# A hybrid diffusion layer on one core: the rest of the modulation summed by VectorE in place of GpSimd

## The chip, the cores and the metric

The kernel runs on one core of a Trainium2 chip. The metric is the device time of one execution in microseconds (us), the median of several runs. The engines are TensorE (PE in the rows; its weight loads are PEld), VectorE (DVE), ScalarE (ACT), GpSimd (POOL) and SyncE (SP), which here only issues DMA transfers. Each engine works through its own queue in order; the queues wait for one another by semaphores.

## The reference, cut to what matters

One layer: a modulated norm and an input projection, a token mixer (differential attention and a gated linear attention, GLA), an output projection, then a mixture of experts and a last norm. The modulation vectors come from one conditioning vector `c`:

```
mod_lat = (silu(c) @ w_ada[layer] + b_ada[layer])[:, None, :]
sh1, sc1, gt1, sh2, sc2, gt2 = split(mod_lat, 6, axis=-1)
h_lat = modulate(rms_norm(x, norm_mix_g), sh1, sc1)
y_lat, _ = token_mixer(h_lat, h_ctx, ...)
x = x + gt1 * y_lat
h2 = modulate(rms_norm(x, norm_ffn_g), sh2, sc2)
x = x + gt2 * hier_moe(h2, ...)
return rms_norm(x, final_norm_g)
```

`w_ada` is 1024 x 6144. The first 2048 columns (`sh1`, `sc1`) are needed before the first projection. The other 4096 (`gt1`, `sh2`, `sc2`, `gt2`) are needed only after the mixer; they are "the rest of the modulation" and the subject of the change.

## The kernel before, in words

All work is f32. A product is made of three matmuls on TensorE, with each operand split into an upper part `hi` (rounded, by ScalarE) and a remainder `lo` (by VectorE, one subtraction); `mm3`, lines 116 to 121, issues them, so that L119, L120 and L121 stand for nearly all multiplications. The input projection is made tile by tile by `bform` (line 446): 128 tokens by 256 (or 288) columns, 8 x 3 = 24 matmuls into a PSUM buffer `acc`, of which there are three. The weights of the projection come in pieces (`wraw`, split by L275 on ScalarE and L276 on VectorE).

The program goes through the projection in stages: GLA values (`gvalue`, 20 tiles), then in one `with` block (lines 664 to 725) the keys and gate ranks (`klr`, 10 tiles), the output gates (`r`, 16 tiles) and the queries (`q`, 8 tiles), then the values and heads of the attention (from line 848). Beside the tiles run "chains", Python generators that emit a few instructions and then yield a delay; a `Weave` ticks them after every few matmuls and so fixes by hand, with the delays of the table `DEL`, the order of the instructions on the four compute engines. SP's queue is not written by hand: a scheduler at build time sets its order.

- `klr_chain` (line 506) makes the decay gates of a tile: ScalarE (L520 to L527), VectorE (m L524, ml L529, ki L546, a copy to `sall` L552) and TensorE take turns.
- `recurrence` (line 563) carries the GLA state from chunk to chunk: dependent operations on VectorE on 64 partitions by 512 (L589, L590).
- An `r` tile: ScalarE makes the gate `gs` (L701 to L703), VectorE multiplies it with `acc` (L707) and so frees the PSUM buffer, SP stores it (L708). `gs` has two buffers. A `q` tile: VectorE multiplies `acc` with `eP` (L721), TensorE transposes the result (L657), ScalarE copies it (L659), SP stores it (L660).
- `ada_rest` (line 595) is the chain that the change touches. It makes the 4096 sums in eight parts (j) of 512 columns. Rows of `w_ada` lie eight to a partition: for each of eight k one block `aw` of 128 x 512 is loaded by SP (L603, 256 KB, three buffers), multiplied on GpSimd by the column `sil[:, 0, k]` (L643) and added to `aacc` (L645; two buffers, and the first block of a part is multiplied straight into it). After the fifth block of a part, `finish` takes up the part before: the sum is split (ah L613 on ScalarE, al L614 on VectorE), summed over the 128 partitions by two matmuls with a column of ones (L617, L618), added to the bias (brow L619) and stored (L620; some parts also in another order, L626, L631, L633). A block's load, `load()`, is emitted behind the block three places before it.

TensorE is thus tied to the chain at two points: the matmuls L617 and L618 stand in its queue and wait for the sum, and SP's queue, which loads `aw`, also carries the stores and loads of the tiles.

Of the kernel before, what the change touches and what calls it, by code (L numbers as in the profile page):

```python
# [20 lines left out]
OP = mybir.AluOpType  # L21
# [54 lines left out]
def f32(ap):  # L76
    return ap.bitcast(F32)
# [3 lines left out]
def body(ctx, tc, io, out, dbg=None):  # L81
    nc = tc.nc
# [166 lines left out]
    sil = hp.tile([P, 2, KD], F32, name="sil")  # L249
# [345 lines left out]
    def ada_rest():  # L595

        ws = []

        def load():
            i = len(ws)  # L600
            if i < 8 * KD:
                ws.append(sp.tile([P, 512], F32, name="aw", bufs=3))
                nc.sync.dma_start(ws[i], wv[:, i % KD, 2048 + i // KD * 512:2048 + (i // KD + 1) * 512])  # L603

        for _ in range(3):
            load()
        accs = {}

        def finish(j):
            acc, brow = accs.pop(j)  # L610
            ah = sp.tile([P, 512], F32R, name="ah", bufs=1)
            al = sp.tile([P, 512], F32R, name="al", bufs=1)
            nc.scalar.activation(ah, acc, AF.Copy)  # L613
            nc.vector.tensor_tensor(al, acc, f32(ah), op=OP.subtract)  # L614
            yield DEL["ar2"]
            ps = pp.tile([P, 512], F32, name="t", bufs=DEL["T"])
            nc.tensor.matmul(ps[:1], ones, ah, start=True, stop=False)  # L617
            nc.tensor.matmul(ps[:1], ones, al, start=False, stop=True)  # L618
            nc.vector.tensor_tensor(brow, ps[:1], brow, op=OP.add)  # L619
            nc.sync.dma_start(dr_mod[:, j * 512:(j + 1) * 512], brow)  # L620
            if j // 2 in (1, 2):
                c0 = j % 2 * 512
                orow = sp.tile([P, 512], F32, name="ah", bufs=1)[:1]
                src, dst = brow.rearrange("o (c k) -> o c k", k=KD), orow.rearrange("o (k c) -> o c k", k=KD)
                if j // 2 == 1:
                    nc.vector.tensor_copy(dst, src)  # L626
                else:
                    gain = sp.tile([P, 512], F32, name="al", bufs=1)[:1]
                    nc.scalar.dma_start(gain, io["ffn_g"][:, c0:c0 + 512])
                    yield DEL["ar2"]  # L630
                    nc.vector.scalar_tensor_tensor(dst, src, 1.0, gain.rearrange("o (c k) -> o c k", k=KD),  # L631
                                                   op0=OP.add, op1=OP.mult)
                nc.sync.dma_start(dr_ord[:, (j // 2 - 1) * 1024:j // 2 * 1024].rearrange(  # L633
                    "o (k c) -> o k c", k=KD)[:, :, j % 2 * 64:j % 2 * 64 + 64], orow.rearrange("o (k c) -> o k c", k=KD))

        for j in range(8):
            acc = sp.tile([P, 512], F32, name="aacc", bufs=2)
            brow = sp.tile([1, 512], F32, name="brow", bufs=2)
            accs[j] = (acc, brow)
            nc.scalar.dma_start(brow, io["b_rest"][:, j * 512:(j + 1) * 512])  # L640
            for k in range(KD):
                w = ws[j * KD + k]
                nc.gpsimd.tensor_scalar(w if k else acc, w, sil[:, 0, k:k + 1], 1.0, op0=OP.mult, op1=OP.mult)  # L643
                if k:
                    nc.gpsimd.tensor_tensor(acc, acc, w, op=OP.add)  # L645
                load()
                yield DEL["ar"]
                if k == 4 and j:
                    yield from finish(j - 1)
        yield DEL["ar1"]  # L650
        yield from finish(7)
# [12 lines left out]
    with tc.manual_schedule(engines=COMPUTE):  # L664
# [11 lines left out]
        nc.vector.tensor_copy(hmR.rearrange("p a b -> p (a b)"), raw[:, 256:456])  # L676
        sums_ps = pp.tile([P, 512], F32, name="sums", bufs=1)
        side.add(ada_rest())
        for t in range(NA):
            ps = bform("klr", t)  # L680
# [914 lines left out]
    with tc.tile_pool(name="ring_c", reuse_waits="tile", bufs=1) as ring_c, \  # L1595
# [170 lines left out]
        with tc.manual_schedule():  # L1766
# [63 lines left out]
            for n in range(2):  # L1830
                c = slice(n * 512, n * 512 + 512)
# [15 lines left out]
    with tc.For_i(0, again, 1):  # L1847
        with tc.tile_pool(name="ov", reuse_waits="tile", bufs=1) as ov, \
                tc.tile_pool(name="ov_ps", reuse_waits="tile", bufs=1, space=PSUM) as op_:

            def til(name, shape, dt=F32):
                return ov.tile([P] + list(shape), dt, name="ov" + name)

            with tc.For_i(0, n_extra, 1) as it:
# [65 lines left out]
                for i, nm in enumerate(("w_gate", "w_up")):  # L1920
                    for hf in range(2):
                        w = til("wt", [4, 512])
# [16 lines left out]
                for hf in range(2):  # L1939
                    w = til("wt", [2, 1024])  # L1940
# [118 lines left out]
```

## Time and profile before

| | |
|---|---|
| median of 3 runs | 1458.75 us (1458.16 to 1459.15) |
| the profiled execution | 1454.76 us, span 1452.9 us from first to last instruction |
| busy share of the span | PE 92%, PEld 76%, DVE 76%, ACT 60%, POOL 30% |
| instructions of DVE and POOL | 1589 and 393 |
| chain that ended last, by engine | PE 61%, DVE 11%, DMA 9%, POOL 7%, ACT 4%, issue 3% |

The times in the rows are from the start of that execution's span. Durations of TensorE are modelled and overlap, since matmuls are pipelined; a new one of 256 columns starts much sooner than the one before is shown to end. "Idle before" and the releaser in brackets tell how long an engine stood and what ended it; a wait for several things is put down to the last. PEclk is the granted clock of TensorE as a share of 2.4 GHz; its lower level is 1.2 GHz.

### The profile page before, as it was taken

What the parts mean: (1) busy time and instruction counts of PE and PEld (TensorE: products, weight loads), DVE (VectorE), ACT (ScalarE), POOL (GpSimd) and SP (SyncE); (2) the same over time, 40 slices, a digit from 0 to 9 for tenths busy, and PEclk for the clock granted to TensorE, in tenths of its full rate; (3) what the DMA queues carried; (4) which work ended last, traced back from release to release, by engine and by line L of the source; (5) the groups of instructions that cost most, each with busy time, mean ns of one, the idle gap of its engine ahead of it and who ended that gap; (6) DMA issues with size and microseconds to landing.
All of it is one profiled execution on the core that took longest, in us unless ns stands there. A gap on an engine that the chain in (4) does not pass through costs nothing.

```text
span 1452.9 us, 21094 instructions
## 1 busy us (share of the span) xinstructions
PE 1332.4 (92%) x7352; PEld 1105.0 (76%) x7352; DVE 1102.2 (76%) x1589; ACT 870.4 (60%) x1458; POOL 437.5 (30%) x393
## 2 busy tenths in 40 slices
PE   6898987899999899999899599999999999999982
PEld 1698886889888788887688467777777777777761
DVE  5553568734765699999556689999999999999975
ACT  6744753223222488888443467777777777777781
POOL 1576578810234434433100202222222222222201
PEclk9799999899999999999999699999999999999996
DMA  8526665676546961512574689999999999999963
GB/s 275 198 91 179 191 202 159 218 244 192 166 149 188 246 184 44 138 44 85 212 260 155 237 330 355 372 369 369 375 378 370 375 363 358 358 372 362 351 268 150
DMA packets 121539, 360.77 MB, mean 248 GB/s; under 512 B 18726, under 2 KB 47422, under 8 KB 98388
## 3 DMA queue, kind: packets, MB, share of 16 engines
q1 hardware_dynamic: 109808, 337.50, 66.4%
q0 software_dynamic: 10080, 20.09, 5.0%
q10 hardware_dynamic: 1540, 1.78, 0.4%
q8 instruction: 59, 0.97, 0.3%
q14 instruction: 52, 0.43, 0.1%
HBM read 318.24 MB, written 58.74 MB: 259 GB/s over the span
## 4 chain that ended last, share of the span: by engine, by line
PE 61%; DVE 11%; DMA 9%; POOL 7%; ACT 4%; issue 3%; SPq 0%; POOLq 0%; DVEq 0%; ACTq 0%
PE acc L119 4%; PE acc L121 4%; PE acc L120 4%; PE y L119 4%; PE y L121 4%; PE y L120 4%; PE u L120 4%; PE u L121 3%; PE g L119 3%; PE g L121 3%; PE u L119 3%; PE g L120 3%; POOL aacc L645 3%; PE y L1676 3%; DVE nm L1037 3%
## 5 line engine op out<-in xcount | busy, mean ns | idle before, releaser
L1628 DVE TENSOR_TENSOR lo<-ring,hi 128x1024 fp32r<-128x1024 f32 x323 | 382.8, 1222 | 43.0 <-ACT hi L1627 28.6
L1627 ACT ACTIVATE hi<-ring 128x1024 fp32r<-128x1024 f32 x323 | 335.7, 1059 | 87.1 <-PE y L121 53.3
L119 PE MATMUL acc<-whi,hThi 128*128 128x256 f32 (+1 forms) x592 | 178.2, 301 | 7.9 <-DVE gs L707 5.4
L121 PE MATMUL acc<-whi,hTlo 128*128 128x256 f32 (+1 forms) x592 | 172.5, 291 | 0.9 <-DVE hTlo L326 0.6
L120 PE MATMUL acc<-wlo,hThi 128*128 128x256 f32 (+1 forms) x592 | 171.9, 290 | 0.4 <-DVE wlo L276 0.3
L119 PEld LDWEIGHTS acc<-whi,hThi 128*128 128x128 f32 x592 | 117.1, 198 | 9.8 <-DVE gs L707 5.8
L121 PEld LDWEIGHTS acc<-whi,hTlo 128*128 128x128 f32 x592 | 116.5, 197 | 2.5 <-DVE hTlo L326 2.1
L120 PEld LDWEIGHTS acc<-wlo,hThi 128*128 128x128 f32 x592 | 116.6, 197 | 2.0 <-DVE wlo L276 0.8
L119 PE MATMUL u<-hi,xh 128*128 128x512 f32 x256 | 100.9, 394 | 3.5 <-ACT hi L1627 3.5
L120 PE MATMUL u<-lo,xh 128*128 128x512 f32 x256 | 100.9, 394 | 3.5 <-DVE lo L1628 3.5
L119 PE MATMUL g<-hi,xh 128*128 128x512 f32 x256 | 103.8, 405 | 0.0
L120 PE MATMUL g<-lo,xh 128*128 128x512 f32 x256 | 100.6, 393 | 0.8 <-DVE lo L1628 0.8
L121 PE MATMUL g<-hi,xl 128*128 128x512 f32 x256 | 100.8, 394 | 0.0
L121 PE MATMUL u<-hi,xl 128*128 128x512 f32 x256 | 100.4, 392 | 0.0
L1037 DVE TENSOR_REDUCE nm<-S 128x1 f32<-128x1280 f32 x64 | 94.9, 1485 | 6.1 <-PE S L1032 6.1
L1032 PE MATMUL S<-kst,qst 128*128 128x512 f32 (+1 forms) x384 | 93.2, 380 | 4.5 <-ACT p L1042 3.4
L1042 ACT ACTIVATE p<-S,nm 128x1280 f32<-128x1280 f32 x64 | 85.0, 1328 | 15.4 <-DVE nm L1037 10.9
L1607 POOL DMA_INDIRECT xg<-dr_h,tok x32 | 45.2, 1414 | 149.7 <-DVE tok L1252 127.7
L119 PE MATMUL y<-hi,th 128*128 128x512 f32 x186 | 85.2, 458 | 0.0
L645 POOL TENSOR_TENSOR aacc<-aacc,aw 128x512 f32<-128x512 f32 x56 | 79.9, 1428 | 4.7
L1032 PEld LDWEIGHTS S<-kst,qst 128*128 128x128 f32 x384 | 66.0, 194 | 17.7 <-ACT p L1042 7.7
L121 PE MATMUL y<-hi,tl 128*128 128x512 f32 x186 | 72.6, 390 | 0.0
(399 smaller groups left out, 3267.5 us busy)
## 6 DMA issues: line engine op xcount, KB each, us to landing
ring<-in_w_down_dram SPq DMA_DIRECT2D x63, 1024.0 KB
ring<-in_w_gate_dram SPq DMA_DIRECT2D x57, 1024.0 KB
ring<-in_w_up_dram SPq DMA_DIRECT2D x57, 1024.0 KB
aw<-in_w_ada_dram SPq DMA_DIRECT2D x64, 256.0 KB
wraw<-in_w_in_dram SPq DMA_DIRECT2D x44, 256.0 KB
wada<-in_w_ada_dram SPq DMA_DIRECT2D x16, 512.0 KB
qst<-dr_q SPq DMA_DIRECT2D x32, 256.0 KB
raw_o<-in_w_gate_dram SPq DMA_DIRECT2D x14, 512.0 KB
```

Source lines behind the costliest of these rows:

```text
L119: nc.tensor.matmul(out_ap, ah, bh, start=start, stop=False)
L120: nc.tensor.matmul(out_ap, ah, bl, start=False, stop=False)
L121: nc.tensor.matmul(out_ap, al, bh, start=False, stop=stop)
L645: nc.gpsimd.tensor_tensor(acc, acc, w, op=OP.add)
L1032: nc.tensor.matmul(S[:, c0:c0 + cn], st["qst"][m][s][:, qt * P:(qt + 1) * P], st["kst"][m][:, c0:c0 + cn], start=(s == 0), stop=(s == 1))
L1037: nc.vector.tensor_reduce(d["nm"][:, m:m + 1], d["S"][m], AX.X, OP.max, negate=True)
L1042: nc.scalar.activation(d["p"][m], d["S"][m], AF.Exp, bias=d["nm"][:, m:m + 1], accum_out=d["sm"][:, m:m + 1])
L1607: nc.gpsimd.indirect_dma_start(out=xgb[e % 3], out_offset=None, in_=dr_h2, in_offset=bass.IndirectOffsetOnAxis(ap=tok[:, o:o + 1], axis=0) ...
L1627: nc.scalar.activation(hi, raw, AF.Copy)
L1628: nc.vector.tensor_tensor(lo, raw, f32(hi), op=OP.subtract)
L1676: nc.tensor.matmul(y[:, n], tf[:, kk - PARTS], ws[kk][:, n * 512:(n + 1) * 512], start=start, stop=stop)
```

## The change

The multiplication by the column and the addition become one operation, scalar_tensor_tensor, on VectorE: aacc = aw x c + aacc. The first block of a part is a tensor_scalar on VectorE. Loads, yields, buffers and `finish` stay. Lines of the kernel behind L641 move down by two: the gate product L707 is L709 after, L721 is L723, L657 is L659.

```diff
             for k in range(KD):
                 w = ws[j * KD + k]
-                nc.gpsimd.tensor_scalar(w if k else acc, w, sil[:, 0, k:k + 1], 1.0, op0=OP.mult, op1=OP.mult)
+                c = sil[:, 0, k:k + 1]
                 if k:
-                    nc.gpsimd.tensor_tensor(acc, acc, w, op=OP.add)
+                    nc.vector.scalar_tensor_tensor(acc, w, c, acc, op0=OP.mult, op1=OP.add)
+                else:
+                    nc.vector.tensor_scalar(acc, w, c, 1.0, op0=OP.mult, op1=OP.mult)
                 load()
                 yield DEL["ar"]
```

The instructions move on three engines. First VectorE's queue in the r tiles, from a brow (L619) on; before:

```order
L619 TENSOR_TENSOR brow<-t,brow 1x512
L626 COPY ah<-brow 1x64x8
L707 TENSOR_TENSOR gs<-gs,acc 128x256
L589 TENSOR_TENSOR sall<-sall 64x512
L590 TENSOR_TENSOR sall<-sall,e_1349 64x512
L589 TENSOR_TENSOR sall<-sall 64x512
L590 TENSOR_TENSOR sall<-sall,e_1349 64x512
L707 TENSOR_TENSOR gs<-gs,acc 128x256 x3
```

and the same place after (L645 and L647 are the new operations):

```order
L709 TENSOR_TENSOR gs<-gs,acc 128x256
L645 SCALAR_TENSOR_TENSOR aacc<-aw,sil,aacc 128x512 x2
L589 TENSOR_TENSOR sall<-sall 64x512
L590 TENSOR_TENSOR sall<-sall,e_1349 64x512
L589 TENSOR_TENSOR sall<-sall 64x512
L590 TENSOR_TENSOR sall<-sall,e_1349 64x512
L709 TENSOR_TENSOR gs<-gs,acc 128x256
L647 TENSOR_SCALAR aacc<-aw,sil 128x512
L645 SCALAR_TENSOR_TENSOR aacc<-aw,sil,aacc 128x512
L709 TENSOR_TENSOR gs<-gs,acc 128x256
L645 SCALAR_TENSOR_TENSOR aacc<-aw,sil,aacc 128x512 x2
L709 TENSOR_TENSOR gs<-gs,acc 128x256
```

The three gates that stood side by side now have two blocks between each pair; the order of VectorE's other operations is unchanged. On GpSimd's queue the 120 operations of L643 and L645 are gone, and only the ten small memsets of `st` (L688) are left between the value stage and the attention's values.

Second, TensorE's queue where the last of the eight sums goes over the partitions (`ah` of the last part; `acc` with numbers, to tell the tiles apart); before, in the first value tile of the attention:

```order
L119 MATMUL acc_3418<-whi_3107,hThi_154 128x256
L120 MATMUL acc_3418<-wlo_3108,hThi_154 128x256
L617 MATMUL t_3393<-ah_3389,ones_75 1x512
L121 MATMUL acc_3418<-whi_3107,hTlo_155 128x256
L119 MATMUL acc_3418<-whi_3107,hThi_154 128x256
```

and after, in the third value tile (the first is acc_3362, the second acc_3412):

```order
L119 MATMUL acc_3447<-whi_3061,hThi_154 128x256
L120 MATMUL acc_3447<-wlo_3062,hThi_154 128x256
L617 MATMUL t_3337<-ah_3333,ones_75 1x512
L121 MATMUL acc_3447<-whi_3061,hTlo_155 128x256
L119 MATMUL acc_3447<-whi_3061,hThi_154 128x256
```

The matmuls of the last sum stand two tiles later in the queue; those of the seventh, and the transposes of the last query tile, about one tile later. TensorE's order is otherwise the same but for one transpose that moves by four matmuls, and ScalarE's is unchanged. On SP's queue the 64 loads of `aw` stand at other places among the same stores and loads.

## Rows read from the trace of the kernel before

**Rows 1.** By stretches: busy us (count) of PE, PEld, DVE, ACT, POOL; PEclk, DMA share, GB/s.

```profile
128.00:188.70 60.70, 55.70 (x402) 50.50 (x403) 33.06 (x54) 43.76 (x105) 39.80 (x44) 1.00 0.58 174
188.70:256.00 67.30, 53.10 (x417) 50.34 (x416) 50.42 (x66) 28.32 (x66) 51.63 (x43) 0.95 0.60 181
256.00:286.80 30.80, 26.62 (x199) 25.93 (x197) 26.02 (x28) 6.29 (x11) 24.46 (x21) 0.88 0.67 216
286.80:303.00 16.20, 11.69 (x82) 10.72 (x81) 5.69 (x10) 4.15 (x8) 7.80 (x9) 0.89 0.62 201
303.00:400.00 97.00, 96.58 (x683) 89.50 (x683) 52.16 (x125) 27.31 (x88) 11.31 (x8) 1.00 0.64 203
```

**Rows 2.** Chain that ended last, 90 to 300 us: shares by line.

```profile
by line: POOL aacc L645 23.2%; POOL aw L643 14.9%; DMA aw<-in_w_ada_dram 11.5%; issue 4.2%; DMA dr_gv<-gvs 3.7%; PE acc L121 3.7%; PE acc L119 3.6%; PE acc L120 3.6%; DMA dr_gs<-gs 3.4%; POOL aacc L643 2.0%; DMA eP<-dr_eP 1.9%; DVE wlo L276
```

**Rows 3.** Groups of GpSimd, 100 to 296 us: busy us, mean ns | idle before.

```profile
L645 POOL TENSOR_TENSOR aacc<-aacc,aw 128x512 f32<-128x512 f32 x56 | 79.9, 1428 | 4.7
L643 POOL TENSOR_SCALAR aw<-aw,sil 128x512 f32<-128x512 f32 x56 | 52.3, 933 | 11.5 <-DMA aw<-in_w_ada_dram 11.5
```

**Rows 4.** Waits of PE, SP and ACT, stages before 305: us, times, longest.

```profile
PE t L617 <- ACT ah L613: 6.4, 5, 3.8
PE acc L119 <- DVE gs L707: 5.4, 2, 4.3
...
SPq L603 <- POOL aacc L645: 61.0, 35, 4.5
...
SPq L708 <- DVE gs L707: 5.1, 3, 4.4
...
ACT gs L701 <- DMA dr_gs<-gs: 27.8, 11, 4.1
```

**Rows 5.** Timeline of DVE, ACT, PE: start us, us [idle before <-releaser].

```profile
252.50 1.98 DVE L631 SCALAR_TENSOR_TENSOR ah<-brow,al 1x512 f32<-1x512 f32 x1
...
254.65 0.38 ACT L701 ACTIVATE gs<-acc 128x256 f32<-128x256 f32 x1 [3.16 <-DMA dr_gs<-gs]
...
254.79 0.58 PE L119 MATMUL acc<-whi,hThi 128*128 128x256 f32 x1 [4.25 <-DVE gs L707]
```

**Rows 6.** Timeline of DVE and POOL around 240 us.

```profile
234.21 1.67 DVE L590 TENSOR_TENSOR sall<-sall,e 64x512 f32<-64x512 f32 x1
...
239.63 0.68 DVE L590 TENSOR_TENSOR sall<-sall,e 64x512 f32<-64x512 f32 x1
240.33 0.69 DVE L589 TENSOR_TENSOR sall<-sall 64x512 f32<-64x512 f32 x1
...
242.70 0.69 POOL L643 TENSOR_SCALAR aw<-aw,sil 128x512 f32<-128x512 f32 x1 [4.58 <-DMA aw<-in_w_ada_dram]
```

**Rows 7.** DVE 128x512 in the timeline, and the group of the gate product.

```profile
144.63 0.68 DVE L546 TENSOR_TENSOR ki<-ki,kk 128x512 f32<-128x512 f32 x1
145.24 0.68 DVE L524 SCALAR_TENSOR_TENSOR m<-g,na 128x512 f32<-128x512 f32 x1
...
L707 DVE TENSOR_TENSOR gs<-gs,acc 128x256 f32<-128x256 f32 x16 | 6.5, 412 | 8.2 <-ACT gs L703 8.2
```

**Rows 8.** Groups of DVE over the whole span, and one cast in the timeline.

```profile
L1055 DVE SCALAR_TENSOR_TENSOR p<-p,kap,p 128x768 f32<-128x768 f32 x32 | 32.3, 1011 | 0.0
...
L1745 DVE SCALAR_TENSOR_TENSOR ring<-ring,n_y,raw_o 128x1024 f32<-128x1024 f32 x8 | 9.7, 1279 | 0.0
...
100.43 0.42 DVE L670 CAST mh<-m 98x512 fp32r<-98x512 f32 x1
```

**Rows 9.** Pieces of the same chain: aw loads, start us, us.

```profile
104.98 2.48 DMA aw<-in_w_ada_dram
...
237.91 4.70 DMA aw<-in_w_ada_dram
```

**Rows 10.** Timeline of PE and ACT at the tail.

```profile
293.96 0.44 PE L617 MATMUL t<-ah,ones 128*1 128x512 f32 x1 [3.83 <-ACT ah L613]
...
300.09 0.38 ACT L862 ACTIVATE dqh<-acc 128x256 fp32r<-128x256 f32 x1 [2.18 <-PE acc L121]
```

## The prediction

> **What bounds the kernel now.** I read the view by stretches first [rows 1]. From 303 to 400 us TensorE is busy 96.58 of 97 us, and the attention and expert stages behind it start only when it gets there: what is won before 303 us comes off the whole time. Between 128 and 303 us TensorE is not full. The work there falls into four stretches: the ten gate tiles ("gate", 128 to 188.7), the sixteen r tiles ("r", to 256), the eight q tiles ("q", to 286.8) and the change-over to the value tiles ("tail", to 303). TensorE is busy 55.70 of 60.70, 53.10 of 67.30, 26.62 of 30.80 and 11.69 of 16.20 us, and in the last three the granted clock sinks to 0.95, 0.88 and 0.89 of 2.4 GHz.
>
> Next, who is late. In the chain of what ended last between 90 and 300 us, the two GpSimd lines of the summation hold 23.2% and 14.9% [rows 2]. Their cost [rows 3]: 79.9 us for 56 additions and 52.3 us for the 56 scalings ahead of them, 132 us or 2.36 us a block, and eight scalings that begin a sum. The waits show how this reaches TensorE [rows 4]. Directly: it waits 6.4 us for the upper half `ah` of a finished sum. Indirectly, by two roads: SP's queue stood 61.0 us behind aw loads whose buffer GpSimd had not freed, and ScalarE waited 27.8 us for stores of `gs` in that queue; and 5.4 us for r tiles' gate products, which free PSUM, when VectorE's queue was late. One such place [rows 5]: ScalarE gets its next `gs` buffer only at 254.65 after 3.16 us, and TensorE starts again at 254.79 after 4.25 us idle, once a gate product is done that stood on VectorE behind recurrence steps and an operation of 1.98 us at 252.50.
>
> **What the change removes.** All 120 operations on GpSimd, and with them a second cost. VectorE's product L590 took 1.67 us at 234.21 and 0.68 us at 239.63; in between GpSimd ran dry (its next scaling starts at 242.70 after 4.58 us of waiting) [rows 6]. So VectorE's long durations are company of GpSimd, not work. Counted with free durations (0.61 us from start to start for independent 128x512 operations, 0.70 for the dependent 64x512 ones, 0.41 for a gate [rows 6, 7]) VectorE's own work in r is 16 gates 6.6, thirteen 128x512 operations 7.9, 22 steps of the recurrence 15.4 and 14 others of finished sums and small steps at 0.55 on average, 7.7: 37.6 us, where it is busy 50.42 [rows 1]. In q it is 14 x 0.61 + 12 x 0.70 and one other of about 1.1, 18.0 us, where it is busy 26.02.
>
> **What it adds.** 56 scalar_tensor_tensor and 8 tensor_scalar on VectorE, 128x512 f32. No row has the first in that shape from SBUF: 128x1024 costs 1.279 us, 128x768 1.011 [rows 8], by the line through both 128x512 costs 0.74; the floor is 0.61, the start distance above, the ceiling 1.011. The 0.74 is nearest, since size scales it. For a tensor_scalar I take 0.42, a cast of 98x512 [rows 8], and no more than 0.74 in any case, which would add 2.6 us over the whole. Sum 56 x 0.74 + 8 x 0.42 = 44.8 us. By the order the 64 blocks lie 2 before the gate tiles, 22 in gate, 24 in r, 12 in q, 4 in the tail. GpSimd ran ahead of its place whenever a load and a sum buffer were there; VectorE takes each block where it stands in the order.
>
> **Stretch by stretch**, with VectorE free of GpSimd:
> - gate: 20 x 0.74 + 2 x 0.42 = 15.6 us on VectorE, which is busy 33.06 of 60.70 now. TensorE is at 55.70, so little can be won. Most blocks fall where VectorE waits for ScalarE, but about one per tile stands ahead of a step of the gate chain (m, ki or ml) on which TensorE waits: at most 10 x 0.74 = 7.4. Against it, ml and ki lose their long durations and 1.3 us of a gate matmul's wait goes. Bounds -5 to +7.4, taken **+1.5**.
> - r: 37.6 + 21 x 0.74 + 3 x 0.42 = 54.4 us on VectorE, just above TensorE's 53.10. Now VectorE is the bound, and what is late next is the reload of an aw buffer. There are three buffers, so a block's load is issued when the block three before it is done; from issue to landing it takes 2.48 to 4.70 us [rows 9], taken 4.5, near the upper end, since the entry may stand behind another on SP. On average three blocks take 54.4 / 8 = 6.8 us, enough. In three places blocks of two gates stand without a recurrence step between, and VectorE needs only 2.0 to 3.0 us for three blocks: 1.5 to 2.5 us late each, 6 in all. So 54.4 + 6 = 60.4 against 67.30: **-6.9**; bounds -12.9 (no wait) and +6 (the durations do not fall).
> - q: 18.0 + 10 x 0.74 + 2 x 0.42 = 26.2 on VectorE, TensorE 26.62; the same late reloads, twice 2, and up to 2 for the eP loads in the same queue: 32.5 against 30.80: **+1.7**; bounds -4.2 and +9.
> - tail: now the last sum reaches TensorE at 293.96 and it waits 3.83 us with the first value tile half done [rows 10]; the third value tile ends near 303, one tile of 24 matmuls (at most 24 x 97 / 683 = 3.4 us by rows 1) after the second is evacuated at 300.09. After the last q product VectorE has one block, al, brow, three blocks, a wait of 0.7 for `ah` and al: 0.74 + 0.61 + 0.61 + 2.2 + 0.7 + 0.69, with 1 for late loads 6.6 us. In the new order the last two matmuls of the sum stand inside the third value tile, two tiles later than now, so TensorE has work meanwhile and ends that tile some 9 us after the last q product, not 16.2: **-7.2**; bounds -8.7 and -3.
>
> The edits with no price of their own: DMA bytes stay as they are. In the value stage ahead of 128 us SP stops less; TensorE's multiplications cover that, and without the cover it would be a gain. GpSimd's memsets for `st` come earlier, off the path. Behind 303 us the other work keeps its order, and TensorE covers it. Sum +1.5 - 6.9 + 1.7 - 7.2 = **-10.9 us**. The profiled execution took 1454.76 us (span 1452.9), 4 us under the median of the runs, so it becomes 1443.9, and the median 1458.75 becomes **1447.9**.
>
> **The rivals.**
> - *The whole gain.* Loads land in time and no chain is lengthened: gate 0, r at 54.4 (-12.9), q at TensorE's 26.6 (-4.2), tail -8.7: -25.8, 1433. For it: average spacing 6.8 us against 4.5. Against it: the bunched blocks.
> - *VectorE's queue replaces GpSimd's.* gate pays its +7.4, r waits 9 (-3.9), q 8 (+3.8), tail -7.2: +0.1, 1459. For it: both engines are within 2 us of each other in r and q, and an in-order queue hands every wait on.
> - *Slower: reloads late throughout.* VectorE stops at a block whose load is still queued on SP, and behind it stand the gate products that free PSUM. 36 blocks of r and q through three buffers are twelve rounds of reload plus 0.74. If a load also lies behind a store held as long as the longest hold of a gate store today, 4.4 us [rows 4], a round is 8.9 + 0.74: 115.7 us against 98.1 now, +17.6, with +1.5 and -7.2 gives +11.9, 1471. It decides from a reload of 7.9 us on, where the rounds eat 98.1 + 5.7. Against it: those holds came from GpSimd being behind.
> - *Slower: VectorE is full and stays so.* If the long durations were its own, r is 50.42 + 16.8 + 6 (+5.9), q 26.02 + 8.2 + 6 (+9.4); with +1.5 and -4 for the tail +12.8, 1472. Row 239.63 speaks against it. The Trainium skill's Perfetto Trace Analysis, section Optimizing Scalar/DVE Operations, points this way: from a saturated VectorE work may go to GpSimd, and since both share an SBUF read port, moving work between them might not help; this change moves it toward the fuller engine. By that rule 1472, by rows 6 the forecast.
> - *It does not do what it says:* the order shows all 64 blocks on VectorE and none on GpSimd, so no chance for this.
>
> **How the numbers follow.** A measurement of this kernel tells 0.2% (2.9 us) from no change. Chances: forecast 0.52 (its own range 1440 to 1453), the whole gain 0.12, VectorE's queue 0.17, late reloads 0.13, VectorE full 0.06. Faster 0.64, same 0.17, slower 0.19. The range 1435 to 1466 leaves out half of the whole gain and some two thirds of the slower cases, about 0.18.
>
> **What would show it.** GpSimd's 132 us gone; 56 blocks of about 0.74 us and 8 of about 0.42; L589 and L590 at 0.7; VectorE nearly full in r (over 54 of some 60 us) with waits on aw loads of a few us; the wait at the last sum gone; r some 7 us and tail some 7 shorter. It is wrong if the recurrence steps stay above 1 us, if VectorE waits over 15 us on aw loads, if gate grows by more than 5, or if what is won before 303 us is lost behind it.

## The result, and the profile after

The changed kernel takes **1444.7 us** (median of 4 runs, 1443.57 to 1445.63) against 1458.95 us of the kernel before (four runs too), a ratio of **0.991** (95% interval 0.989 to 0.993). Timed once more beside other kernels it took 1443.06 us against 1456.7, again 0.991 (0.989 to 0.993). The profiled execution took 1444.24 us with a span of 1442.4, 10.5 us less than the profiled one of before. Forecast were 1447.9 us, and -10.9 us between profiled executions.

Behind the edited lines the numbers grow by 2: the gate product L707 is now L709, ScalarE's first step on an r tile L701 is L703, the q product L721 is L723, and the evacuation of a value tile L862 and L863 is L864 and L865. By the stretches of [rows 1], each ending at the same work as before (columns as there: busy us and count of PE, PEld, DVE, ACT, POOL; the last two rows cover what follows):

```profile
126.70:189.30 62.60, 58.09 (x410) 52.45 (x409) 43.09 (x76) 44.26 (x106) 0.70 (x7) 0.97 0.60 190
189.30:247.80 58.50, 49.64 (x397) 47.13 (x396) 50.99 (x90) 27.93 (x65) 1.95 (x3) 0.94 0.68 199
247.80:278.90 31.10, 27.49 (x237) 26.66 (x236) 26.11 (x41) 7.40 (x13) 0.00 (x0) 1.00 0.86 263
278.90:287.40 8.50, 7.05 (x53) 6.36 (x53) 6.53 (x11) 2.93 (x6) 0.00 (x0) 1.00 0.57 190
287.40:300.00 12.60, 9.84 (x66) 9.26 (x67) 5.00 (x11) 2.19 (x5) 0.00 (x0) 0.86 0.91 290
300.00:400.00 100.00, 99.58 (x679) 91.21 (x678) 55.24 (x131) 28.80 (x96) 14.62 (x10) 1.00 0.61 193
```

Gate went from 60.7 to 62.6 us, r from 67.3 to 58.5, q from 30.8 to 31.1, the tail from 16.2 to 8.5: +1.9 - 8.8 + 0.3 - 7.7 = -14.3 us. The tail ends 15.6 us earlier (287.4 against 303.0), as the gate stretch also began 1.3 us earlier. But from 287.4 to 300 us TensorE is busy only 9.84 of 12.6 us, at a granted clock of 0.86 of 2.4 GHz, and gets through 66 matmuls; in the 12.6 us behind the tail of the kernel before (303.0 to 315.6) it was busy throughout, at a granted clock of 1.00, and got through 102. A part of the gain is lost there.

The chain that ended last, 90 to 300 us, which before held GpSimd's two lines with 40% (first blocks included) [rows 2]:

```profile
by line: PE acc L119 10.3%; PE acc L121 10.1%; PE acc L120 10.1%; DMA aw<-in_w_ada_dram 7.0%; DVE aacc L645 6.6%; issue 6.3%; DMA dr_gs<-gs 5.0%; PE g L550 4.5%; DMA wraw<-in_w_in_dram 2.8%; DMA eP<-dr_eP 2.3%; DMA dr_v<-dqh 2.3%; PE g L537
```

VectorE's recurrence in the kernel before, 128 to 303 us (busy us, mean ns | idle before):

```profile
L590 DVE TENSOR_TENSOR sall<-sall,e 64x512 f32<-64x512 f32 x18 | 21.5, 1192 | 0.6
L589 DVE TENSOR_TENSOR sall<-sall 64x512 f32<-64x512 f32 x16 | 17.7, 1108 | 0.1
```

and VectorE's groups after, 100 to 303 us, which answer to [rows 3, 6]:

```profile
L645 DVE SCALAR_TENSOR_TENSOR aacc<-aw,sil,aacc 128x512 f32<-128x512 f32 x56 | 41.7, 744 | 4.0 <-DMA aw<-in_w_ada_dram 3.6
L276 DVE TENSOR_TENSOR wlo<-wraw,whi 128x512 fp32r<-128x512 f32 (+1 forms) x24 | 16.8, 700 | 15.5 <-ACT whi L275 15.1
L590 DVE TENSOR_TENSOR sall<-sall,e 64x512 f32<-64x512 f32 x18 | 12.4, 686 | 0.6
L589 DVE TENSOR_TENSOR sall<-sall 64x512 f32<-64x512 f32 x16 | 10.9, 682 | 0.1
...
L529 DVE TENSOR_TENSOR ml<-m,mh 128x512 fp32r<-128x512 f32 x10 | 6.9, 687 | 2.9 <-ACT mh L527 2.8
```

An addition costs 0.744 us, and the steps of the recurrence take 0.68 to 0.69 us where their means were 1.11 and 1.19 us. The waits of SP's queue, ScalarE and TensorE, 100 to 303 us, against [rows 4]:

```profile
SPq L603 <- DVE aacc L645: 28.7, 31, 5.2
...
SPq L603 <- DVE gs L709: 8.3, 8, 3.4
...
ACT gs L703 <- DMA dr_gs<-gs: 14.6, 7, 4.2
ACT dqh L864 <- DMA dr_v<-dqh: 9.9, 3, 8.6
...
PE t L618 <- DVE al L614: 5.1, 4, 2.6
PE acc L119 <- DVE dql L865: 3.9, 2, 2.6
PE t L617 <- ACT ah L613: 2.9, 3, 1.5
```

[rows 4] begin at 128 us. From 100 us SP stood 66.2 us on the blocks' loads behind the additions in the kernel before, where the first of these rows has 28.7. New on SP are 8.3 us in which a load of a block stands behind a gate product in VectorE's queue. ScalarE waits 14.6 us for its `gs` buffers in place of 27.8. New before 303 us is the wait at `dqh` and `dql`, the evacuation of the value tiles. The timeline shows it:

```profile
284.69 0.39 ACT L864 ACTIVATE dqh<-acc 128x256 fp32r<-128x256 f32 x1 [0.28 <-issue]
285.50 0.38 ACT L864 ACTIVATE dqh<-acc 128x256 fp32r<-128x256 f32 x1
294.99 0.38 ACT L864 ACTIVATE dqh<-acc 128x256 fp32r<-128x256 f32 x1 [8.60 <-DMA dr_v<-dqh]
...
295.88 0.58 PE L119 MATMUL acc<-whi,hThi 128*128 128x256 f32 x1 [2.58 <-DVE dql L865]
```

TensorE ran ahead of the evacuations until no PSUM buffer was free, and waited 2.58 us. The evacuations of the kernel before (all twenty, then the third) and of the changed kernel (all twenty):

```profile
L862 ACT ACTIVATE dqh<-acc x20: 376/384/386, 297.0 to 363.7; 128x256 fp32r<-128x256 f32 x20
...
307.31 0.39 ACT L862 ACTIVATE dqh<-acc 128x256 fp32r<-128x256 f32 x1 [6.32 <-DMA dr_v<-dqh]
...
L864 ACT ACTIVATE dqh<-acc x20: 377/384/386, 284.7 to 352.8; 128x256 fp32r<-128x256 f32 x20
```

The first comes 12.3 us earlier than before, the third too, and the last 10.9 us earlier. The third waited for a store in both kernels.

### The profile page after: what moved, and what is told of

Read it like the earlier page. It is cut to its first block, busy times and chain, and to the rows that moved or that the text cites. A ratio compares the mean times of both kernels' runs of the same rounds, so it can differ in the third digit from the quotient of the medians.

```text
span 1442.4 us, 21048 instructions
## 1 busy us (share of the span) xinstructions
PE 1331.0 (92%) x7352; PEld 1104.1 (77%) x7352; DVE 1115.2 (77%) x1653; ACT 870.6 (60%) x1458; POOL 298.7 (21%) x273
## 4 chain that ended last, share of the span: by engine, by line
PE 68%; DVE 13%; DMA 7%; ACT 5%; issue 4%; POOL 2%; SPq 0%; ACTq 0%; POOLq 0%; DVEq 0%
PE acc L119 5%; PE acc L120 5%; PE acc L121 5%; PE y L119 4%; PE y L121 4%; PE y L120 4%; PE u L120 4%; PE g L120 4%; PE u L121 4%; PE g L121 4%; PE g L119 4%; PE u L119 4%; PE y L1678 4%; DVE nm L1039 3%; PE S L1034 2%
## 5 line engine op out<-in xcount | busy, mean ns | idle before, releaser
L120 PE MATMUL y<-lo,th 128*128 128x512 f32 x186 | 72.5, 390 | 0.0
```

Of the source, the lines that this page charges most:

```text
L120: nc.tensor.matmul(out_ap, ah, bl, start=False, stop=False)
```

## The experiments

**Theory:** most of the gain is that VectorE's own operations lose the company of GpSimd, which had made them long. **Rivals:** the gain is GpSimd's slow chain no longer holding load buffers and SP's queue; or it belongs to the tail alone, where the last sum stood in TensorE's way.

Profiled executions also differ ahead of the gate tiles and behind the start of the attention, where no edit aimed: ScalarE's first evacuation of a gate tile (`kk`) falls between 122.8 and 128.1 us in these fourteen profiles (124.7 and 122.8 in two of the changed kernel), and from the first attention score to the end of the span they take 964.0 to 971.6 us. So the kernels are compared from the one of these two landmarks to the other. For the kernel before these rows give 126.0 and 483.8, 357.8 us between, for the changed kernel 124.7 and 472.8, 348.1 us between:

```profile
L684 ACT ACTIVATE kk<-acc x10: 367/378/387, 126.0 to 180.3; 128x256 f32<-128x256 f32 x10
...
L1032 PE MATMUL S<-kst,qst x384: 276/393/722, 483.8 to 670.8; 128*128 128x512 f32 x128, 128*128 128x256 f32 x64
...
L686 ACT ACTIVATE kk<-acc x10: 365/378/387, 124.7 to 180.3; 128x256 f32<-128x256 f32 x10
...
L1034 PE MATMUL S<-kst,qst x384: 276/393/629, 472.8 to 659.9; 128*128 128x512 f32 x128, 128*128 128x256 f32 x64
```

In between stand the first `gs`, the first q product and the first `dqh`, which cut the stretches of the table. They are not those of [rows 1], in which the expectations count: the r tiles of the changed kernel are 58.5 us there and 63.5 here, those of the kernel before 67.3 and 70.6. Us by stretch, then median and ratio of the timed runs:

| kernel | gate tiles | r tiles | q tiles and change-over | values to attention | sum | median | ratio (95%) |
|---|---|---|---|---|---|---|---|
| before | 59.7 | 70.6 | 40.7 | 186.8 | 357.8 | 1456.7 to 1458.95 | 1 |
| changed | 61.0 | 63.5 | 35.5 | 188.1 | 348.1 | 1444.7 | 0.991 (0.989 to 0.993) |
| the same again | 61.0 | 63.8 | 36.5 | 187.0 | 348.3 | 1443.1 | 0.991 (0.989 to 0.993) |
| idle work on GpSimd | 65.7 | 89.4 | 40.4 | 186.7 | 382.2 | 1478.5 | 1.015 (1.013 to 1.018) |
| scaling alone | 62.1 | 69.1 | 35.1 | 188.3 | 354.6 | 1447.8 | 0.993 (0.991 to 0.995) |
| adding alone | 74.0 | 83.4 | 35.2 | 187.8 | 380.4 | 1473.6 | 1.010 (1.009 to 1.012) |
| thin sum | 58.4 | 59.6 | 32.4 | 188.1 | 338.5 | 1433.7 | 0.984 (0.982 to 0.986) |
| first 3 sums on GpSimd | 59.7 | 63.7 | 36.5 | 188.6 | 348.5 | 1443.8 | 0.991 (0.989 to 0.993) |
| last 5 sums on GpSimd | 60.6 | 71.8 | 41.5 | 186.8 | 360.7 | 1455.5 | 0.999 (0.998 to 1.001) |
| four buffers | 61.1 | 62.2 | 36.4 | 186.4 | 346.1 | 1438.9 | 0.987 (0.986 to 0.989) |
| table late | 61.0 | 63.1 | 35.7 | 186.3 | 346.1 | 1440.9 | 0.988 (0.987 to 0.990) |
| both | 60.6 | 62.9 | 34.9 | 186.0 | 344.4 | 1439.3 | 0.989 (0.987 to 0.991) |
| both, blocks closer | 61.1 | 65.5 | 33.6 | 188.1 | 348.3 | 1440.7 | 0.988 (0.986 to 0.989) |
| both, rows by GpSimd | 61.0 | 61.5 | 36.1 | 186.1 | 344.7 | 1441.0 | 0.989 (0.987 to 0.990) |

The changed kernel, profiled twice, repeats its sum to 0.2 us, single stretches to 1.1; the kernel before and each of the others were profiled once. By this the change is worth 9.5 to 9.7 us between the landmarks.

**Idle work on GpSimd.** The bias rows lie in the first row of two 128x512 tiles, whose rows 64 to 127 are the scratch.

```diff
+                nc.gpsimd.tensor_scalar(dm[1], dm[0], h_, 1.0, op0=OP.mult, op1=OP.mult)
+                nc.gpsimd.tensor_tensor(dm[0], dm[0], dm[1], op=OP.add)
                 load()
```

> The changed kernel, with GpSimd given its old 128 operations back as idle work: at each block a scaling and an adding of 64x512 zeros in scratch rows, on which nobody waits. The sum stays on VectorE. Theory (most of the gain is VectorE's own operations getting back to their undisturbed durations): VectorE's 64x512 and 128x512 operations in the stretch of the recurrence go from 0.69 us back to 1.0 to 1.2 us, the 56 summing operations from 0.75 to 1.0 us or more, the stretch of the r units grows by 8 to 15 us, and the time is 1455 to 1470 us, as slow as the kernel before or slower. Rival (the gain is that GpSimd's slow chain no longer releases the load buffers and the gate products): nobody waits for GpSimd here either, so the time stays at 1443 to 1447 us.

These are 128 idle operations; the kernel before had 120 there. It took 1478.5 us, 34 us more than the changed kernel, beyond the theory's own upper end. Groups of 120 to 310 us:

```profile
L654 POOL TENSOR_TENSOR bb<-bb,bb 64x512 f32<-64x512 f32 x58 | 89.0, 1534 | 4.8
L653 POOL TENSOR_SCALAR bb<-bb,sil 64x512 f32<-64x512 f32 x57 | 63.0, 1105 | 5.6
L649 DVE SCALAR_TENSOR_TENSOR aacc<-aw,sil,aacc 128x512 f32<-128x512 f32 x50 | 56.1, 1123 | 0.4
L590 DVE TENSOR_TENSOR sall<-sall,e 64x512 f32<-64x512 f32 x18 | 19.4, 1079 | 0.6
L589 DVE TENSOR_TENSOR sall<-sall 64x512 f32<-64x512 f32 x16 | 18.3, 1142 | 0.1
```

and by stretches, from the first `gs` to the first q product:

```profile
190.40:279.80 89.40, 64.45 (x463) 61.30 (x462) 84.42 (x95) 32.38 (x73) 83.77 (x63) 0.85 0.48 143
```

Nobody waits for this work, and yet the recurrence is back at 1.08 to 1.14 us, a summing operation takes 1.12 us, and VectorE is busy 84.42 of 89.40 us. So the company of GpSimd is shown as a cost by itself, and the rival that leaves it out falls. The run is no copy of the kernel before: there VectorE does not have the sum as well. Nor does it divide the 9.5 to 9.7 us: what part of them came from the operations' own durations, and what part from load buffers and SP's queue freed sooner, no run separates.

**Scaling alone, adding alone.** The same with one of the two lines.

> The kernel with idle work on GpSimd, but with the scaling alone: 64 operations of 64x512 at the places of before, no adding. With both, 33.9 us more than in the changed kernel passed from the start of the gate stretch to the attention (382.2 against 348.1 to 348.3 us), for 63.0 us of scaling and 89.0 us of adding on GpSimd. Theory (VectorE is disturbed for as long as GpSimd works, whatever GpSimd does): the damage goes by GpSimd's time, 8 to 18 us, and the time is 1452 to 1462 us. Rival (the adding, which reads two operands, is what disturbs): 0 to 4 us and 1442 to 1448 us.

> The same with the adding alone: 64 idle operations of 64x512 with two operands, no scaling. Theory (VectorE is disturbed for as long as GpSimd works): 14 to 24 us more than the changed kernel, 1458 to 1468 us. Rival (only the adding disturbs): nearly the whole damage, 28 to 34 us, 1471 to 1478 us.

Against 348.2 us the scaling costs 6.4 us, the adding 32.2, nearly all of the 34 of both. For the adding the rival holds; for the scaling the 6.4 us lie between the two, and the median, 1447.8 us, just inside the rival's bounds. The idle operations keep their places in GpSimd's queue, but as they wait for no block they run ahead of the sum: the last scaling starts at 208.2 us and the last adding at 240.6. By stretch their numbers are alike (32 scalings and 29 additions in the gate tiles, 25 and 27 in the r tiles), so one operation can be set against the other. VectorE's groups of 120 to 340 us, with scaling alone:

```profile
L649 DVE SCALAR_TENSOR_TENSOR aacc<-aw,sil,aacc 128x512 f32<-128x512 f32 x55 | 44.5, 810 | 4.3 <-DMA aw<-in_w_ada_dram 3.9
...
L529 DVE TENSOR_TENSOR ml<-m,mh 128x512 fp32r<-128x512 f32 x10 | 7.3, 733 | 3.0 <-ACT mh L527 2.8
```

and with adding alone:

```profile
L653 POOL TENSOR_TENSOR bb<-bb,bb 64x512 f32<-64x512 f32 x55 | 86.0, 1564 | 4.3
L649 DVE SCALAR_TENSOR_TENSOR aacc<-aw,sil,aacc 128x512 f32<-128x512 f32 x55 | 55.0, 999 | 4.5 <-DMA aw<-in_w_ada_dram 4.1
...
L529 DVE TENSOR_TENSOR ml<-m,mh 128x512 fp32r<-128x512 f32 x10 | 11.8, 1176 | 2.9 <-ACT mh L527 2.8
...
L552 DVE COPY sall<-g 128x512 f32<-128x512 f32 x10 | 6.8, 680 | 0.7 <-PE g L550 0.7
L524 DVE SCALAR_TENSOR_TENSOR m<-g,na 128x512 f32<-128x512 f32 x10 | 6.8, 680 | 0.0
...
L651 DVE TENSOR_SCALAR aacc<-aw,sil 128x512 f32<-128x512 f32 x7 | 6.6, 939 | 0.0
```

`ml`, made in the gate tiles from two operands in SBUF, goes from 0.69 to 1.18 us beside the additions and to 0.73 beside the scalings, though GpSimd is busy for much the same share of these tiles (43.8 of 74.0 us with additions, 31.6 of 62.1 with scalings). `m`, with one operand in PSUM, and the copy out of PSUM stay at 0.68 beside the same additions. The Trainium skill, SBUF — State Buffer, section Who interferes with whom, says that a VectorE instruction contends with GpSimd when it has two inputs in SBUF and GpSimd reads SBUF, and that one with at most one SBUF input, outside the two-port modes, does not. The rows of L649 and L529 (two tensors in SBUF, stretched) and of L552 and L524 (one operand in PSUM, not stretched) agree. The first block of a part, L651, reads one tensor in SBUF and a column, and it is stretched too, from 0.48 to 0.94 us; in which mode it runs no row shows. Of a difference between GpSimd's scaling and its adding that section says nothing; here it is 6.4 against 32.2 us.

**Thin sum.**

```diff
-                    nc.vector.scalar_tensor_tensor(acc, w, c, acc, op0=OP.mult, op1=OP.add)
+                    nc.vector.scalar_tensor_tensor(acc[:, :8], w[:, :8], c, acc[:, :8], op0=OP.mult, op1=OP.add)
```

> The changed kernel with the 56 adding operations cut to the first 8 of 512 columns, so most of the sum over rows is left out; loads, order and waits are kept. It gives the price of the work on VectorE. Theory (VectorE's 41.7 us are hidden behind the matmuls except in the stretch of the r units, where VectorE is busy 51.0 of 58.5 us): 3 to 8 us faster than the changed kernel, 1437 to 1442 us, most of it in the r units, which can't fall below their 49.6 us of matmuls. Rival 1 (all 41.7 us hidden): 1443 to 1446 us. Rival 2 (the loads set the pace, not VectorE): also 1443 to 1446 us, with VectorE idle on the blocks' loads for more than the 4 us of now.

The additions, 120 to 310 us:

```profile
L645 DVE SCALAR_TENSOR_TENSOR aacc<-aw,sil,aacc 128x8 f32<-128x8 f32 x55 | 12.0, 218 | 7.4 <-DMA aw<-in_w_ada_dram 7.1
```

9.7 us less by the sums, 9 to 11 by the medians: more than the theory gave. And the saving does not sit in the r units alone: gate 2.6, r 3.9 to 4.2, q and change-over 3.1 to 4.1. So the sum still costs something in each stretch: about a third of the 29 us that were taken off VectorE. The time, 1433.7 us, rules out both rivals. The sign that the second named did come, in part: with VectorE lighter, its waits for blocks grow from 3.9 to 9.9 us (7.1 at these additions, 2.8 at the first blocks).

**First and last sums on GpSimd.** `j < 3`, or `j >= 3`, decides which engine takes a block:

```diff
-                if k:
+                if j < 3:
+                    nc.gpsimd.tensor_scalar(w if k else acc, w, c, 1.0, op0=OP.mult, op1=OP.mult)
+                    if k:
+                        nc.gpsimd.tensor_tensor(acc, acc, w, op=OP.add)
+                elif k:
                     nc.vector.scalar_tensor_tensor(acc, w, c, acc, op0=OP.mult, op1=OP.add)
```

> The blocks of the first three sums of eight (24 of 64, those of the gate stretch) go to GpSimd as in the kernel before, the other 40 stay on VectorE. By stretch, the changed kernel was 1.9 us slower in the gate stretch and 8.8 us faster in the r units. Theory (each stretch pays for itself, VectorE being disturbed only while GpSimd works): the gate stretch is back at 60 to 61 us, the r units stay at 58 to 61 us, and the time is 1441 to 1446 us. Rival (GpSimd falls behind in the gate stretch and its backlog reaches into the r units, as it does in the kernel before): the r units take 62 us or more and the time is 1448 to 1456 us.

> The other way round: the blocks of the first three sums on VectorE, the other 40 on GpSimd as in the kernel before. Theory (the gain belongs to the stretches from the r units on, where GpSimd disturbs VectorE and ends the tail): the r units take 65 to 69 us again, the tail about 16 us, and the time is 1454 to 1461 us, the kernel before or a little slower. Rival (half of the gain comes from GpSimd having no backlog at the start of the r units): the r units take 61 to 64 us and the time is 1448 to 1453 us.

Both as the theory said, by the times and by the table set against the changed kernel and the kernel before. With the first sums on GpSimd the gate tiles are back at 59.7 us and the r tiles stay at 63.7; of the 1.3 us won the sum, 348.5 us, shows nothing. With the last ones there, r takes 71.8 us, q and change-over 41.5, as in the kernel before, and the gain is gone. The recurrence of this last run, 120 to 310 us:

```profile
L590 DVE TENSOR_TENSOR sall<-sall,e 64x512 f32<-64x512 f32 x18 | 22.7, 1261 | 0.6
L589 DVE TENSOR_TENSOR sall<-sall 64x512 f32<-64x512 f32 x16 | 18.2, 1135 | 0.1
```

The gain belongs to the 40 blocks behind the gate tiles, about 7 us of it to the r tiles and 4 to 5 to the q tiles and the change-over, so the tail alone does not account for it either.

**Four buffers.** The room comes from the bias row, loaded later into one buffer.

```diff
-                ws.append(sp.tile([P, 512], F32, name="aw", bufs=3))
+                ws.append(sp.tile([P, 512], F32, name="aw", bufs=4))
...
+            brow = sp.tile([1, 512], F32, name="brow", bufs=1)
+            nc.scalar.dma_start(brow, io["b_rest"][:, j * 512:(j + 1) * 512])
```

> The changed kernel with four buffers for the blocks in place of three (the room is taken from the bias row, which has one buffer in place of two and is loaded when a sum is finished). It tests the term of the late reloads, for which the prediction took 6 us in the r units, while the trace after shows VectorE waiting 4.0 us for blocks in all. Theory (the term was too large): 0 to 3 us faster, 1441 to 1445 us, with VectorE's waits for blocks under 1.5 us. Rival (the reloads hold more than the waits show, by SyncE's queue, which stands 28 us behind the summing operations): 4 to 8 us faster, 1437 to 1441 us.

The additions, 120 to 310 us:

```profile
L645 DVE SCALAR_TENSOR_TENSOR aacc<-aw,sil,aacc 128x512 f32<-128x512 f32 x55 | 40.9, 743 | 0.5
```

VectorE's waits for blocks fall from 4.0 to 0.5 us, and 2.1 us are won up to the attention: the theory's size. The median fell by 4 to 6 us, as the rival said; the kernel with both edits, below, decides between them.

**Table late.**

```diff
-        nc.scalar.dma_start(rope, io["rope"])
...
+                if (i, t) == (0, 6):
+                    nc.scalar.dma_start(rope, io["rope"])
```

> The changed kernel with the load of the 1 MB rotation table moved from ahead of the value tiles to behind the seventh of them. After the tail the trace shows 4.6 us of the gain given back between 287 and 353 us, where ScalarE waits 8.6 us at 295 us for a store of values that was issued at 290 us. Theory (the table's load, which now starts at 284 us, takes the transfer time from the loads and stores of that stretch): the wait falls under 3 us and the time falls by 2 to 4.5 us, to 1440 to 1443 us. Rival (SyncE's queue, which stands 5.2 us on the last row of the sum before it can issue the stores, holds them): the wait stays at 6 us or more and the time at 1443 to 1446 us.

The third evacuation of a value tile:

```profile
293.32 0.38 ACT L863 ACTIVATE dqh<-acc 128x256 fp32r<-128x256 f32 x1 [8.18 <-DMA dr_v<-dqh]
```

2.1 us by the sums and a median inside the theory's bounds, but not by the wait that it named: that stands at 8.2 us, as the rival said. How the 2.1 us came is open; single stretches repeat only to 1.1 us.

**Both, and the changed kernel again beside it.**

> The changed kernel itself, timed again beside the next kernels so that they stand against the same runs. All theories: 1443 to 1447 us, a ratio of 0.990 to 0.992.

> The changed kernel with both earlier edits: four buffers for the blocks, and the rotation table loaded behind the seventh value tile. Alone they gave 1438.9 and 1440.9 us; against the changed kernel the first matmul of the attention scores started 1.2 us and 3.0 us earlier. Theory (the two are local and add up, and what the four buffers gave beyond 1.2 us arose behind the attention and is not theirs): the attention starts 3.5 to 5 us earlier than in the changed kernel and the time is 1438 to 1442 us. Rival (all that was measured is theirs, and adds up): 1434 to 1437 us.

From gate tiles to attention 344.4 us, 3.8 less than the changed kernel: 2.1 and 2.1 nearly add up. The time, 1439.3 us, is 3.7 less than the changed kernel's on the same chip. The local theory holds; four buffers are not worth 6 us. It is the best version found by the sums, 0.25% under the changed kernel, though the intervals of the two ratios still overlap. Here the third `dqh` comes at 291.01 and waits for TensorE, not for a store:

```profile
291.01 0.38 ACT L863 ACTIVATE dqh<-acc 128x256 fp32r<-128x256 f32 x1 [7.83 <-PE acc L121]
```

**Both, blocks closer,** with `ar` at 1.0.

> The kernel with both edits (four buffers, table late), and the distance between two blocks of the sum cut from 1.15 to 1.0 in the order's units, so that some 13 per cent of the blocks move forward, out of the r and q units into the gate stretch, where VectorE is busy 40.9 of 60.6 us against 53.9 of 62.9 us in the r units. Theory (what is left of the sum's cost lies in the r units, where VectorE is nearly full): from the start of the gate stretch to the attention 2 to 4 us less than the 344.4 us of the kernel with both edits, and a time of 1435 to 1438 us. Rival (the gate stretch has no room either, since its waits go through VectorE as well): 0 to 2 us more, 1439 to 1442 us.

The gate and the r tiles of this run:

```profile
123.90:185.00 61.10, 56.70 (x398) 51.18 (x398) 40.97 (x72) 42.77 (x103) 0.69 (x7) 0.97 0.57 181
185.00:250.50 65.50, 56.74 (x438) 54.24 (x437) 54.59 (x95) 32.85 (x74) 1.89 (x3) 0.92 0.63 196
```

VectorE has 72 operations in the gate stretch, as many as without the edit, and 95 in r, also as many. So no block moved into the gate tiles, and the run tells nothing of its question. What it does show: up to the change-over TensorE waits 8.0 us for `al` where it waited 4.0, its granted clock in the r tiles is 0.92 where it was 1.00, and 3.9 us are lost by the sums. That the places of the finished sums did this is likely, not shown.

**Both, rows by GpSimd.**

```diff
-            nc.sync.dma_start(dr_mod[:, j * 512:(j + 1) * 512], brow)
+            nc.gpsimd.dma_start(dr_mod[:, j * 512:(j + 1) * 512], brow)
```

and the same for the reordered rows.

> The kernel with both edits (four buffers, table late), with the stores of the finished rows of the modulation issued by GpSimd, which has next to nothing left to do there, in place of SyncE, whose queue stands 8.8 us on those rows and 7.1 us on the reordered ones, with the loads of blocks and the stores of the gate products behind them. Theory (these stands delay loads that someone waits for): 1 to 3 us less than the 344.4 us from the start of the gate stretch to the attention, and 1436 to 1438.5 us. Rival (the buffers cover them): 0 to 1 us and 1438.5 to 1441 us.

344.7 against 344.4 us, and 1441.0: the rival. From 180 to 370 us the stands on the rows, 15.9 us, are gone, but the queue now stands longer on the blocks' loads: behind a gate product 15.8 us in place of 7.4, behind an addition 19.1 in place of 13.0. So here the wait taken out of this queue was handed to the entries behind it.

## Why the prediction was right, point by point

- **The direction and the cause.** "So VectorE's long durations are company of GpSimd, not work" was read from two rows [rows 6] and is shown by the idle-work run. With it falls the rival that VectorE is full and stays so, toward which the Trainium skill's Perfetto Trace Analysis, section Optimizing Scalar/DVE Operations, had been read: moving the work to the fuller engine did help here, with 0.68 against 1.1 to 1.2 us in the recurrence.
- **The prices.** The addition, 0.74 taken, measured 0.744. The scaling of 128x512, 0.42 taken, measured 0.48: 0.5 us on eight.
- **Gate +1.5:** +1.9 by its own stretch, +1.3 by landmarks, and back at 59.7 us with the first sums on GpSimd.
- **r -6.9:** -8.8 measured. VectorE's bill was 3.4 us too high (54.4 against 50.99 busy), with nearly the counts taken (25 blocks for 24). Operations overlap more than the bill had it: an addition starts 0.67 us ahead of the next operation and a gate product 0.33, where 0.74 and 0.41 were taken, as the timeline shows (2.8 us on 22 and 16):

```profile
238.03 0.75 DVE L645 SCALAR_TENSOR_TENSOR aacc<-aw,sil,aacc 128x512 f32<-128x512 f32 x1
238.70 0.41 DVE L709 TENSOR_TENSOR gs<-gs,acc 128x256 f32<-128x256 f32 x1
239.03 0.68 DVE L614 TENSOR_TENSOR al<-aacc,ah 128x512 fp32r<-128x512 f32 x1
```

  Besides, "6 in all" for late reloads was too much: in r VectorE waits 2.1 us for blocks (3.9 with all stretches, of 11 forecast), and the rest of its idle time there comes mostly from ScalarE's steps. Four buffers removed 3.5 us of those waits and gained 2.1. So two terms of the r sum were too large, the bill by 3.4 us and the reloads by 3.9, and some 5.4 us of other idle time stood in no term: that it came within 1.9 us is in part luck. The sign "over 54 of some 60 us" did not come, VectorE was busy 50.99 of 58.5.
- **q +1.7:** +0.3, on a bill that was nearly exact (26.2 against 26.11 us, though with 13 blocks in place of 12). Of the 6 us taken for late loads VectorE waited 4.2: 1.6 for blocks, 2.6 for `eP`.
- **Tail -7.2:** -7.7. The wait of 3.83 us [rows 10] is 0.20 at the same matmul now.
- **"Behind 303 us the other work keeps its order, and TensorE covers it": this step failed.** The stretches gave -14.3 us and the part up to the attention only -9.7. 4.6 us were lost, 3.3 of them because TensorE had only run ahead on value tiles that could not be evacuated yet (15.6 us earlier there, the first evacuation 12.3), the rest during the later value tiles; in the second profile those took 1.1 us less. The prediction had named this as a sign of being wrong ("if what is won before 303 us is lost behind it"), and it came true of a third of the gain. So that the forecast of -10.9 is near the 9.5 to 9.7 us up to the attention is luck: terms 3.4 us too small met a loss that it did not have.
- **Medians.** 13.6 to 14.3 us between the medians, 9.5 to 9.7 us up to the attention. The rest, some 4 us, has the size by which profiles differ in parts that no edit touched; whether the change has a part in it was not settled.

## What to carry to other kernels

Before moving work onto a busy engine, find in the trace one of its operations at a moment when the other engine is dry, and make its bill from that duration: 0.68 in place of 1.67 us decided this case. Then check that what TensorE gains can be evacuated behind the stretch, for run-ahead that ends in full PSUM is no gain. And to judge an edit of a few us, compare between two landmarks around it, not whole executions.

## What was not expected of the hardware

GpSimd's two kinds of operation are not alike as company: 64 two-operand additions (1.56 us each) cost the kernel 32.2 us, 64 scalings (0.98 us) 6.4, in like numbers by stretch, with at most 0.7 us of waiting for either. VectorE's operations with an operand in PSUM kept their durations; the stretched ones read SBUF alone, two tensors (`ml`, 0.69 to 1.18 us) or, in a part's first block, one tensor and a column (0.48 to 0.94). And both engines pay: GpSimd's scaling of a block takes 0.69 us where it had waited and so ran alone [rows 6]; the idle one of 64x512 takes 0.98 beside VectorE's sum and 1.11 us in the run with both.
